# A hybrid attention and retention layer on one core: a reordered opening with lo parts on GpSimd, the samples' values as the stationary side of their product, and a last store cut in parts

## The chip, the cores and the metric

The kernel runs on one NeuronCore of a Trainium2 chip, as one program. The metric is device time of one execution in microseconds (us). Engines are named as in the profile: PE (TensorE, with its weight loads as PEld), DVE (VectorE), ACT (ScalarE), POOL (GpSimd) and SP (SyncE, whose queue issues the DMAs here). Each engine takes its own instructions in the order in which the program gives them and waits where an operand isn't ready.

## What is computed

One layer, one inference step, for a prompt of 512 tokens, 32 sample tokens (8 sequences of 4) and 16 meta tokens, which share all weights. The model width is 2048 and everything is float32. Cut to what matters:

```python
u = einsum('btd,de->bte', rms_norm(h, norm_g), w_in)            # 2048 -> 12800 columns
qa, ka, va, za, qr, kr, vr, zr, ga, gr = split(u)
# A: sliding-window attention, 16 heads of 64, 4 KV heads, learned sinks, 16 meta tokens always visible
p = exp(s - m) / (sum(exp(s - m)) + exp(sink - m));   o_a = p @ v
# B: retention, 8 heads, key 128, value 256, chunks of 128, state S
S_new = exp(c * lg) * S + einsum('bjhd,bjhe->bhde', k * wk, v)
y_a = (o_a * silu(za)) @ w_pa
y_r = ((group_norm(o_r) * gn_g + gn_b) * silu(zr)) @ w_pr
y = h + (sigmoid(ga) * y_a + sigmoid(gr) * y_r) @ w_o
```

A sample's query sees 128 cached keys of its own sequence, the new keys of the samples and the 16 meta tokens. Outputs are `y` for prompt and samples, the last key and value windows, and the retention states. The 48 rows of sample and meta tokens that all samples' products share are called the shared rows below.

## The kernel before

**Numbers in two parts.** A product of float32 matrices is made of three passes over rounded operands: each operand is split into hi (a rounded copy, by ACT) and lo (the rest, by a subtraction, mostly on DVE), and PE adds hi·hi, hi·lo and lo·hi. `split` (L156 to L158) does this for weights (tile `wspl`, 128x512 at a time) and `make_x` for the normed input (`xh`, `xl`, L231 to L244). Some small products run as plain float32, which the trace shows as two PE instructions for each matmul.

**Jobs.** The work is a list of jobs, each of 128 output columns: a job's weights are loaded in two halves (`run_load`, `wraw`), split in four steps (`run_split`), multiplied over 16 blocks k of the contraction (`run_mm`, L471, tile `pproj`), and evacuated. Side work (heads of attention, samples, retention) stands in generators that emit a piece between blocks: `clock` counts the blocks and a `yield n` lets n of them pass. So the order of PE is written by the program: where a piece waits for another engine, everything behind it on PE waits too. Later jobs are pairs that use seven products in place of eight (`Pair`, L410); they are not changed.

**The opening** (`start`, L246). The tokens arrive in five groups: 0 to 3 are 128 prompt tokens each, 4 holds the samples and the meta tokens. A group is squared and summed (`sq`, L208 to L212, two parts on ACT and two on DVE), its scale is formed (`norm`, L218 and L199; the power runs on POOL), and its four parts are scaled (L223 on ACT, L225 on DVE). `make_x(k, half)` transposes block k of groups 0 and 1 (half 0, 256 columns) or 2 to 4 (half 1, 304 columns). The first job `j0` runs half 0 first, while groups 2 to 4 are normed between its blocks by a table `plan`; then come half 1 of three blocks, eight blocks of half 0 of the second job `j1` (`j1.ahead = 8`), and half 1 of `j0`. Six buffers `spl` hold the split weights.

**The heads** (`k_side`, L627; `pair_side`, L680) transpose the keys or queries of two heads: blocks of 128 tokens, then the 32 or 48 rows of samples and meta tokens as a smaller transposition (`pke`, `pqe`), and for the keys three of 16 rows (L638) among the large ones.

**The samples** (`sample_work`, L795; `sample_side`, L844). For each of the 8 sequences, the scores of all heads stand on 128 rows (4 KV groups of 32). Their transposed probabilities are the stationary side, 32 columns for one group at a time: L837 multiplies with the cached values (128 rows), L838 with the shared rows (48 rows), into `spo`. When all are done, `os` copies the sum, four transpositions (`pf`) turn it, and 32 small products on DVE (L875) gate it into `oas`.

**Retention** (`ret_side`, L958). The meta tokens' state is one plain float32 product over 32 rows (L1069, from `kmt` and `vmt`).

**The end** (`out_side`, L1487): two jobs' columns are transposed back (`pout`), the residual is added, and the rows are stored; for the last pair this follows its last step.

Of the kernel before, what the change touches and what calls it, by code (L numbers as in the profile page):

```python
# [15 lines left out]
P = 128  # L16
# [94 lines left out]
def hybrid_step(ctx: ExitStack, tc: tile.TileContext, A, O):  # L111
# [101 lines left out]

    def norm(i):
# [3 lines left out]
        nc.vector.tensor_reduce(out=r, in_=ss[:, i], axis=AX.X, op=ALU.add)  # L218
        rsqrt(r, r, 1.0 / D, 1e-6, 1)
# [26 lines left out]
    def start(j0, j1):  # L246
# [10 lines left out]
        load_ext()  # L257
        load_x(3)
        run_load(j1, 1)
# [5 lines left out]
        for i in range(2):  # L265
            for c in range(4):
                sq(i, c)
            norm(i)
        for j in (j0, j1):
            j.cuts = ((0, 256), (256, TF))  # L270
# [3 lines left out]
        plan = {2: "20 21", 4: "22 23", 6: "n2", 9: "40 41", 10: "42 43", 11: "n4", 14: "30 31", 15: "32 33"}  # L274
        for k in range(NK):
# [4 lines left out]
            for o in plan.get(k, "").split():  # L280
                if o[0] == "n":
                    norm(int(o[1]))
# [12 lines left out]
        for k in range(j1.ahead):  # L295
            run_mm(j1, k, (0,))
        for k in range(NK):
# [3 lines left out]
            if k in (8, 13):  # L301
                run_split(j1, {8: 2, 13: 3}[k])
# [24 lines left out]
    class Job:  # L327
        def __init__(self, w, c0, nk, rhs, n, evac, pre=None, need=None, kdone=None):
            self.w, self.c0, self.nk, self.rhs, self.n, self.evac = w, c0, nk, rhs, n, evac
            self.pre, self.need, self.kdone, self.cuts, self.ahead = pre, need, kdone, None, 0  # L330
            self.banked, self.tile = False, None
# [110 lines left out]
    def run_split(job, s, eng=nc.vector):  # L442
# [5 lines left out]
        wt = spl.tile([P, 2, 4, P], F32R, tag="spl", name="wspl")  # L448
        hi, lo = wt[:, 0], wt[:, 1]
# [177 lines left out]
    def k_side(n, raw):  # L627
# [5 lines left out]
        for i in range(4):  # L633
# [3 lines left out]
            if i < 3:  # L637
                nc.tensor.transpose(o[:, c + P:c + 144], kt[NS:48, 4], ident[NS:48, NS:48])  # L638
        tr(pe[:, :48], kt[:48, 4], 48)
# [40 lines left out]
    def pair_side(i, raw, get_sz):  # L680
# [8 lines left out]
        tr(pe[:, :NS], kt[:NS, 4], NS)  # L689
# [105 lines left out]
    def sample_work(bb, st):  # L795

        for b in range(bb, 8, 2):
# [32 lines left out]
            nc.vector.tensor_copy(PT[:48, P:256], pT[:48, P:256])  # L830
            yield 4
            if "po" not in st:
                st["po"] = psb("spo")
            po = st["po"]
            for g in range(4):
                o = po[32 * g:32 * g + 32, 64 * b:64 * b + 64]
                nc.tensor.matmul(o, PT[:, 32 * g:32 * g + 32], vcv[:, bb, 64 * g:64 * g + 64], start=True, stop=False)  # L837
                nc.tensor.matmul(o, PT[:48, P + 32 * g:P + 32 * g + 32], vx[:, 64 * g:64 * g + 64],  # L838
# [738 lines left out]
```

## Time and profile before

| | |
|---|---|
| median of 3 runs | 1842.52 us (1841.9 to 1843.4) |
| the profiled execution's own time | 1842.39 us |
| its span (first to last instruction) | 1840.5 us |
| PE busy | 1810.9 us, 98% of the span |
| DVE, ACT, POOL busy | 66%, 40%, 9% |

Busy time of PE is modelled, since matmuls overlap; the chain of waits gives an instruction only what it adds to the chain, which is what is used for sums. A group `L837 PE MATMUL spo<-kvc,sPT` reads: line, engine, operation, tile written, tiles read. In the timeline a row ends with the idle time before it and what ended it. PEclk in the table of windows is the share of full TensorE clock that was granted.

### The profile page before, as it was taken

To read this page: it belongs to the slowest core of one execution; us is meant where nothing else is said; L and a number is where in the kernel's file an instruction comes from. 1 tells how busy PE (TensorE), PEld (TensorE's weight loads), DVE (VectorE), ACT (ScalarE), POOL (GpSimd) and SP (SyncE) were. 2 spreads that over 40 slices of the span, in tenths; PEclk is the share of its full clock that TensorE was granted. 3 is DMA by queue.
4 is the path that set the end of the run, shared out by engine and by line. 5 is a ranking of instruction groups with operands and counts; after the bars stand their busy time and mean duration, and the time that the engine had idled before them with its cause. 6 is when DMAs were issued, how large, how long until landed. Compare 5 with 4: busy or idle time off the path is not lost.

```text
span 1840.5 us, 35155 instructions
## 1 busy us (share of the span) xinstructions
PE 1810.9 (98%) x14483; PEld 1767.5 (96%) x14483; DVE 1219.8 (66%) x2191; ACT 731.4 (40%) x1297; POOL 173.5 (9%) x240
## 2 busy tenths in 40 slices
PE   5999999999999999999999999999999999999999
PEld 4999999988999999999999999999999999999998
DVE  5636666645556555545697767777676678799776
ACT  5535555433323222233344444444444333344332
POOL 1100101100223212222000000000000000120000
PEclk8999999999999999999999999999999999999999
DMA  6232133231534443434454554444447764564553
GB/s 189 73 99 64 52 103 85 75 106 42 180 103 130 133 132 110 126 108 137 146 149 141 151 148 126 117 123 127 143 140 251 228 184 146 153 177 129 141 141 96
DMA packets 358368, 239.53 MB, mean 130 GB/s; under 512 B 12320, under 2 KB 332224, under 8 KB 358176
## 3 DMA queue, kind: packets, MB, share of 16 engines
q1 hardware_dynamic: 358208, 237.29, 44.1%
q8 instruction: 114, 1.87, 0.4%
q14 instruction: 46, 0.38, 0.1%
HBM read 197.27 MB, written 41.88 MB: 130 GB/s over the span
## 4 chain that ended last, share of the span: by engine, by line
PE 92%; DVE 3%; DMA 2%; ACT 1%; issue 1%; SPq 1%; POOL 0%; DVEq 0%; ACTq 0%
PE pproj L471 43%; PE pp L410 38%; PE ro L1137 1%; PE pp L471 1%; DVE wspl L158 1%; PE po L764 1%; DMA qdc<-c_qdec 1%; PE pout L154 0%; PE pT L154 0%; DVE ml L158 0%; PE rso L1097 0%; PE px L154 0%; PE rsu L1103 0%; PE psc L721 0%; PE pM L154 0%
## 5 line engine op out<-in xcount | busy, mean ns | idle before, releaser
L471 PE MATMUL pproj<-xh,wspl 128*128 128x272 f32 (+3 forms) x3840 | 714.6, 295 | 2.0 <-ACT xh L242 2.0
L158 DVE TENSOR_TENSOR wspl<-wraw,wspl 128x512 fp32r<-128x512 f32 (+1 forms) x492 | 465.0, 950 | 218.4 <-ACT wspl L157 215.6
L471 PEld LDWEIGHTS pproj<-xh,wspl 128*128 128x128 f32 x3840 | 567.4, 190 | 11.1 <-issue 4.8
L157 ACT ACTIVATE wspl<-wraw 128x512 fp32r<-128x512 f32 (+1 forms) x492 | 389.0, 804 | 371.5 <-DVE wraw L368 156.7
L471 PE MATMUL pproj<-xl,wspl 128*128 128x272 f32 (+3 forms) x1920 | 405.1, 290 | 1.0 <-DVE xl L243 1.0
L471 PEld LDWEIGHTS pproj<-xl,wspl 128*128 128x128 f32 x1920 | 305.4, 189 | 1.8 <-DVE xl L243 1.8
L410 PE MATMUL pp<-xfh,wspl 128*128 128x272 f32 x1280 | 246.2, 287 | 0.0
L410 PEld LDWEIGHTS pp<-xfh,wspl 128*128 128x128 f32 x1280 | 202.7, 188 | 0.0
L410 PE MATMUL pp<-xh,wspl 128*128 128x272 f32 x960 | 187.6, 288 | 0.0
L410 PE MATMUL pp<-xfl,wspl 128*128 128x272 f32 x640 | 162.8, 287 | 0.0
L410 PEld LDWEIGHTS pp<-xh,wspl 128*128 128x128 f32 x960 | 153.0, 188 | 0.0
L410 PE MATMUL pp<-fh,wspl 128*128 128x272 f32 x768 | 146.3, 288 | 0.2 <-ACT wspl L157 0.2
L410 PE MATMUL pp<-xl,wspl 128*128 128x272 f32 x480 | 123.0, 288 | 0.0
L410 PEld LDWEIGHTS pp<-fh,wspl 128*128 128x128 f32 x768 | 121.2, 188 | 0.6 <-ACT wspl L157 0.3
L410 PEld LDWEIGHTS pp<-xfl,wspl 128*128 128x128 f32 x640 | 120.7, 189 | 0.0
L410 PE MATMUL pp<-fl,wspl 128*128 128x272 f32 x384 | 98.1, 288 | 0.0
L410 PEld LDWEIGHTS pp<-xl,wspl 128*128 128x128 f32 x480 | 90.3, 188 | 0.0
L471 PE MATMUL pproj<-fh,wspl 128*128 128x272 f32 x512 | 84.9, 287 | 0.0
L368 DVE TENSOR_TENSOR wraw<-wraw 128x1024 f32<-128x1024 f32 x64 | 78.0, 1219 | 0.0
L410 PE MATMUL pp<-ofh,wspl 128*128 128x272 f32 x384 | 75.3, 290 | 0.0
L410 PEld LDWEIGHTS pp<-fl,wspl 128*128 128x128 f32 x384 | 72.3, 188 | 0.0
L471 PEld LDWEIGHTS pproj<-fh,wspl 128*128 128x128 f32 x512 | 72.2, 188 | 0.0
(314 smaller groups left out, 2445.9 us busy)
## 6 DMA issues: line engine op xcount, KB each, us to landing
wraw<-w_in SPq DMA_DIRECT2D x200, 512.0 KB
wraw<-w_branch_ret SPq DMA_DIRECT2D x32, 512.0 KB
wraw<-w_out SPq DMA_DIRECT2D x32, 512.0 KB
state<-state_ret SPq DMA_DIRECT2D x16, 512.0 KB
o_ret_sample<-state SPq DMA_DIRECT2D x16, 512.0 KB
wraw<-w_branch_attn SPq DMA_DIRECT2D x16, 512.0 KB
m1l<-m_scr SPq DMA_DIRECT2D x20, 272.0 KB
r_scr<-rprime SPq DMA_DIRECT2D x16, 272.0 KB
```

Of the source, the lines that this page charges most:

```text
L157: nc.scalar.activation(out=hi, in_=src, func=AF.Copy)
L158: eng.tensor_tensor(out=lo, in0=src, in1=hi.bitcast(F32), op=ALU.subtract)
L368: eng.tensor_tensor(out=out, in0=a, in1=b, op=ALU.add)
L410: nc.tensor.matmul(job.ps[bank], w[:, k], job.rhs(form, k)[q], start=fresh and i == 0, stop=i == len(seq) - 1, skip_group_check=True)
L471: nc.tensor.matmul(ps[h][:, :c1 - c0], w, x[:, c0:c1], start=a, stop=e)
L764: nc.tensor.matmul(o, src, PT[:, j * 256 + rh:j * 256 + rh + P], start=("s", j) not in st, stop=False, skip_group_check=True)
L1137: nc.tensor.matmul(o, w[:, cs], x, start=q == 0, stop=q == 5)
```

## The change

**The opening.** The second half of `j1`'s weights is loaded before group 3, not after it. The lo parts of `j0`'s last three splits and `j1`'s first three go to POOL. `j1`'s last two splits get buffers of their own (`wspk`, borrowed from the attention's `kk`), so that all four exist before `j0` ends, and all 16 blocks of `j1`'s half 0 run before half 1 begins. A group's scale (`rstd`) is formed apart from its scaling (`norm`), and the table `plan` is new.

**The heads.** The rows of samples and meta tokens are transposed as a full block of 128, and the three small transpositions of the keys follow the large ones.

**The samples.** The values become the stationary side (128 columns: two KV groups at once) and the probabilities move, 32 columns. The shared rows are multiplied once for all samples, from a tile `spx` in which each sample puts its probabilities. The result is already turned, so `os` and `pf` go, and 16 products on DVE replace the 32.

**Retention.** The meta tokens' state comes from three products of hi and lo parts (`kst`, `kml`, `vst`, `vml`).

**The end.** The last pair has its own function, which stores its columns in parts.

```diff
-    def norm(i):
-        n = P if i < 4 else 48
+    def rstd(i):
         r = xrs[:, i:i + 1]
         nc.vector.tensor_reduce(out=r, in_=ss[:, i], axis=AX.X, op=ALU.add)
         rsqrt(r, r, 1.0 / D, 1e-6, 1)
...
         load_ext()
+        run_load(j1, 1)
         load_x(3)
-        run_load(j1, 1)
...
+        j1.spare = 2
...
-        plan = {2: "20 21", 4: "22 23", 6: "n2", 9: "40 41", 10: "42 43", 11: "n4", 14: "30 31", 15: "32 33"}
+        plan = {4: "20 21", 7: "22 23", 9: "r2", 10: "n2 40 41", 12: "42 43", 13: "r4 30 31", 14: "n4 32", 15: "33"}
...
             if k in (1, 5, 8):
-                run_split(j0, {1: 1, 5: 2, 8: 3}[k])
-            if k in (11, 13):
-                run_split(j1, {11: 0, 13: 1}[k])
-        norm(3)
+                run_split(j0, {1: 1, 5: 2, 8: 3}[k], nc.gpsimd)
+            if k in (9, 11, 13):
+                run_split(j1, {9: 0, 11: 1, 13: 2}[k], nc.gpsimd)
+        rstd(3)
         for k in range(NK - LAG, NK):
             run_mm(j0, k, (0,))
+        j1.ahead = 16
+        run_split(j1, 3)
+        norm(3)
+        for k in range(j1.ahead):
+            run_mm(j1, k, (0,))
         for k in range(3):
             make_x(k, 1)
-        j1.ahead = 8
-        for k in range(j1.ahead):
-            run_mm(j1, k, (0,))
...
-            if i < 3:
-                nc.tensor.transpose(o[:, c + P:c + 144], kt[NS:48, 4], ident[NS:48, NS:48])
-        tr(pe[:, :48], kt[:48, 4], 48)
+        tr(pe[:, :P], kt[:, 4])
+        for i in range(3):
+            c = 144 * (i % 2) + P
+            nc.tensor.transpose(pk[i // 2][:, c:c + 16], kt[NS:48, 4], ident[NS:48, NS:48])
...
-        tr(pe[:, :NS], kt[:NS, 4], NS)
+        tr(pe[:, :P], kt[:, 4])
...
-            for g in range(4):
-                o = po[32 * g:32 * g + 32, 64 * b:64 * b + 64]
-                nc.tensor.matmul(o, PT[:, 32 * g:32 * g + 32], vcv[:, bb, 64 * g:64 * g + 64], start=True, stop=False)
-                nc.tensor.matmul(o, PT[:48, P + 32 * g:P + 32 * g + 32], vx[:, 64 * g:64 * g + 64],
-                                 start=False, stop=True)
+            for q in range(2):
+                nc.tensor.matmul(pov[:, q, b], vcv[:, bb, P * q:P * q + P], ptv[:, q, :, 0:16],
+                                 start=first and q == 0, stop=False, skip_group_check=True)
...
+        for q in range(2):
+            nc.tensor.matmul(po[:, 256 * q:256 * q + 256], vx[:, P * q:P * q + P], st["px"][:48, 256 * q:256 * q + 256],
+                             start=False, stop=True, skip_group_check=True)
...
-        nc.tensor.matmul(pu[:, :256], kmt[96:128], vmt[96:128])
+        for q, (w, x) in enumerate(((kst, vst), (kst, vml), (kml, vst))):
+            nc.tensor.matmul(pu[:, :256], w[96:128], x[96:128], start=q == 0, stop=q == 2)
...
+    def out_last(n, y, x):
+        ...
+        yield 3
+        nc.vector.tensor_tensor(out=x[0][:, :512], in0=pt[:, 0], in1=x[0][:, :512], op=ALU.add)
+        nc.sync.dma_start(O["y_prompt"][0, 0:256, cs].rearrange("(b p) c -> p b c", p=P), r3(x[0][:, :512], 256))
+        for j in (1, 0):
+            while not done.get("last") and j == 0:
+                yield 1
+            ...
+            nc.vector.tensor_tensor(out=xv, in0=r3(pt[:, 0, :256], P), in1=xv, op=ALU.add)
+            nc.sync.dma_start(O["y_prompt"][0, 256:512, cs][:, c].rearrange("(b p) c -> p b c", p=P), xv)
+            nc.vector.tensor_tensor(out=x[2][:NS, c], in0=pt[:NS, 1, :P], in1=x[2][:NS, c], op=ALU.add)
+            nc.sync.dma_start(ysm[:, n * P + P * j:n * P + P * j + P], x[2][:NS, c])
...
+            if n == NK - 2:
+                if s == 5:
+                    side_add(out_last(n, t["y"], t["x"]), 4)
+                if s == 6:
+                    done["last"] = True
+            elif s == 6:
                 side_add(out_side(n, t["y"], t["x"]), 4)
```

Three places, as the instructions stand on an engine. First POOL in the opening, from the memory fills to the first head's key norm (`xrs` is a group's scale, `wspl` and `wspk` are lo parts of weights). Before:

```order
L590 MEMSET qz 128x1024
L199 ISA
L199 TENSOR_TENSOR xrs<-xrs,nhalf 128x1 x5
L601 MEMSET kt 128x128
L199 TENSOR_TENSOR rs<-rs,nhalf 128x10
```

And now:

```order
L199 TENSOR_TENSOR xrs<-xrs,nhalf 128x1 x2
L158 TENSOR_TENSOR wspl<-wraw,wspl 128x512 x3
L199 TENSOR_TENSOR xrs<-xrs,nhalf 128x1
L158 TENSOR_TENSOR wspl<-wraw,wspl 128x512 x2
L199 TENSOR_TENSOR xrs<-xrs,nhalf 128x1
L158 TENSOR_TENSOR wspk<-wraw,wspk 128x512
L199 TENSOR_TENSOR xrs<-xrs,nhalf 128x1
L609 MEMSET kt 128x128
```

Six subtractions of 128x512 stand among the powers that give the scales of groups 2, 4 and 3, each of which must run before DVE can scale that group.

Second DVE, from the scaling of group 2 to the first `xl` of half 1. Before:

```order
L225 TENSOR_SCALAR xext<-xext,xrs 48x512 x3
L158 TENSOR_TENSOR wspl<-wraw,wspl 128x512
L243 SCALAR_TENSOR_TENSOR xl<-px,gains,xh 128x256
L158 TENSOR_TENSOR wspl<-wraw,wspl 128x512
L211 SCALAR_TENSOR_TENSOR xjunk,xss<-xin 128x512 x2
L218 TENSOR_REDUCE xrs<-xss 128x1
L198 TENSOR_SCALAR xrs<-xrs 128x1
L225 TENSOR_SCALAR xin<-xin,xrs 128x512 x3
L243 SCALAR_TENSOR_TENSOR xl<-px,gains,xh 128x304 x12
```

And now:

```order
L228 TENSOR_SCALAR xin<-xin,xrs 128x512 x3
L211 SCALAR_TENSOR_TENSOR xjunk,xss<-xext 48x512
L246 SCALAR_TENSOR_TENSOR xl<-px,gains,xh 128x256 x2
L211 SCALAR_TENSOR_TENSOR xjunk,xss<-xext 48x512
L216 TENSOR_REDUCE xrs<-xss 128x1
L198 TENSOR_SCALAR xrs<-xrs 128x1
L211 SCALAR_TENSOR_TENSOR xjunk,xss<-xin 128x512
L228 TENSOR_SCALAR xext<-xext,xrs 48x512 x3
L211 SCALAR_TENSOR_TENSOR xjunk,xss<-xin 128x512
L216 TENSOR_REDUCE xrs<-xss 128x1
L198 TENSOR_SCALAR xrs<-xrs 128x1
L158 TENSOR_TENSOR wspk<-wraw,wspk 128x512
```

The last two `xl` of half 0, which PE's blocks 14 and 15 need, now stand behind the scaling of group 2, and one split stands ahead of the scaling of group 3; the other splits are gone from DVE.

Third PE, the end of one sample's product with the values and what follows it. Before (the pair of L837 and L838 stands four times in a row, once for each KV group; its last time is shown):

```order
L837 MATMUL spo<-kvc,sPT 32x64
L838 MATMUL spo<-vx,sPT 32x64
L154 MATMUL pkc<-ident,kvc 128x128 x2
L471 MATMUL pproj<-xh,wspl 128x280 x2
L471 MATMUL pproj<-xl,wspl 128x280 x2
```

And now:

```order
L849 MATMUL spo<-sPT,kvc 128x32 x2
L154 MATMUL pkc<-ident,kvc 128x128 x2
L479 MATMUL pproj<-xh,wspl 128x280 x2
L479 MATMUL pproj<-xl,wspl 128x280 x2
L479 MATMUL pproj<-xh,wspl 128x280 x2
```

Eight matmuls for each sample, alternating between 128 and 48 rows, became two of 128 rows; the shared rows' two matmuls stand once, behind the last sample.

More of the change, by code (lines that the diff above doesn't have):

```diff
@@ L212, in sq @@
                                            op1=ALU.mult, accum_out=ss[:n, i, c:c + 1])
+    def rstd(i):
+        r = xrs[:, i:i + 1]
+        nc.vector.tensor_reduce(out=r, in_=ss[:, i], axis=AX.X, op=ALU.add)
+        rsqrt(r, r, 1.0 / D, 1e-6, 1)
     def norm(i):
@@ L330, in __init__ @@
             self.pre, self.need, self.kdone, self.cuts, self.ahead = pre, need, kdone, None, 0
-            self.banked, self.tile = False, None
+            self.banked, self.tile, self.spare = False, None, 0
             self.ps, self.raw = None, None
@@ L447, in run_split @@
         src = r3(job.raw[s // 2], P)[:, 4 * (s % 2):4 * (s % 2) + 4]
-        wt = spl.tile([P, 2, 4, P], F32R, tag="spl", name="wspl")
-        hi, lo = wt[:, 0], wt[:, 1]
+        if s < 4 - job.spare:
+            wt = spl.tile([P, 2, 4, P], F32R, tag="spl", name="wspl")
+            hi, lo = wt[:, 0], wt[:, 1]
+        else:
+            hi, lo = (r3(att.tile([P, TF], F32R, tag="kk", name="wspk", bufs=8)[:, :512], P) for _ in range(2))
         split(hi, lo, src, eng)
@@ L849, in sample_side @@
             yield
-        st = {"n": 0}
+        st = {"n": 0, "px": slot(name="spx")}
         for bb in range(2):
@@ L1047, in ret_side @@
             tr(pb[:, n * P:n * P + P], reps[1 + n])
-        vst, vmt = r1k(F32R, "vst"), r1k(name="vmt")
+        vst, vml = r1k(F32R, "vst"), r1k(F32R, "vml")
         nc.scalar.activation(out=vst, in_=pb[:, :256], func=AF.Copy)
@@ L1051, in ret_side @@
         nc.vector.tensor_tensor(out=vst[r], in0=pb[r, :256], in1=vst[r].bitcast(F32), op=ALU.subtract)
-        nc.scalar.activation(out=vmt[96:128], in_=pb[96:128, :256], func=AF.Copy)
+        r = slice(96, 128)
+        nc.vector.tensor_tensor(out=vml[r], in0=pb[r, :256], in1=vst[r].bitcast(F32), op=ALU.subtract)
         px = psb("rx")
@@ L1485, in out_load @@
         return x + [xs]
+    def out_last(n, y, x):
+        cs = slice(n * P, n * P + 256)
+        pt = psmain("pout")
+        for b in range(2):
+            for j in range(2):
+                tr(pt[:, 0, 256 * b + P * j:256 * b + P * j + P], y[j][:, P * b:P * b + P])
+        yield 3
[4 more added lines that the diff above has]
+                yield 1
+            pt = psmain("pout")
+            c = slice(P * j, P * j + P)
+            for b in range(2):
+                tr(pt[:, 0, P * b:P * b + P], y[j][:, 256 + P * b:256 + P * b + P])
+            tr(pt[:NS, 1, :P], y[j][:, SEQ:TC])
+            xv = r3(x[1][:, :512], 256)[:, :, c]
+            nc.vector.tensor_tensor(out=xv, in0=r3(pt[:, 0, :256], P), in1=xv, op=ALU.add)
+            nc.sync.dma_start(O["y_prompt"][0, 256:512, cs][:, c].rearrange("(b p) c -> p b c", p=P), xv)
+            nc.vector.tensor_tensor(out=x[2][:NS, c], in0=pt[:NS, 1, :P], in1=x[2][:NS, c], op=ALU.add)
+            nc.sync.dma_start(ysm[:, n * P + P * j:n * P + P * j + P], x[2][:NS, c])
     def out_side(n, y, x):
```

49 lines of the change are left out of this document (20 added, 29 removed).

## The prediction

> **What bounds the kernel now.** I read the page first, its busy times and its chain of waits, then who waited for whom on PE.
>
> ```profile
> PE 1810.9 (98%) x14483; PEld 1767.5 (96%) x14483; DVE 1219.8 (66%) x2191; ACT 731.4 (40%) x1297; POOL 173.5 (9%) x240
> PE 92%; DVE 3%; DMA 2%; ACT 1%; issue 1%; SPq 1%; POOL 0%; DVEq 0%; ACTq 0%
> ```
>
> ```profile
> PE px L154 <- DVE xin L225: 9.5, 3, 3.3
> PE pproj L471 <- ACT xh L242: 2.0, 1, 2.0
> PE ru L1069 <- ACT vmt L1052: 1.1, 1, 1.1
> ```
>
> PE is the bound: 92% of the chain is its own work, and apart from the opening it waits for almost nothing (1.1 us at the first head's state is the longest). No row names a weight load. So an instruction less on PE is time less, as long as the engines behind it keep up. The opening is different. The timeline of PE there, and the granted clock of two stretches in the table of windows (start and end, width, then busy times, then PEclk):
>
> ```profile
> 25.66 0.44 PE L154 MATMUL px<-ident,xin 128*128 128x128 f32 x2 [1.80 <-DVE xl L243]
> 31.59 0.39 PE L471 MATMUL pproj<-xh,wspl 128*128 128x256 f32 x1 [2.02 <-ACT xh L242]
> 35.89 0.47 PE L154 MATMUL px<-ident,xin 128*128 128x128 f32 x1 [2.93 <-DVE xin L225]
> 43.41 0.53 PE L471 MATMUL pproj<-xh,wspl 128*128 128x256 f32 x2
> 43.78 0.30 PE L471 MATMUL pproj<-xl,wspl 128*128 128x304 f32 x1
> 43.92 0.30 PE L471 MATMUL pproj<-xh,wspl 128*128 128x304 f32 x1
> ```
>
> ```profile
> 19.80:33.30 13.50, 8.37 (x60) 6.92 (x58) 12.04 (x33) 9.94 (x25) 1.10 (x2) 1.00 0.83 222
> 33.50:43.50 10.00, 7.61 (x32) 6.46 (x33) 3.90 (x11) 2.26 (x4) 0.70 (x2) 0.50 0.19 55
> ```
>
> Three gaps, 6.75 us together, and the clock at 0.50 for 10 us after the second: 7.61 us of work there cost about 3.8 us extra. DVE was busy 12.04 of 13.5 us in the stretch with the gaps: PE waits for it. The first 304-column product, where `j0`'s half 1 begins, is the second of the two in the row of 43.41, at about 43.6 us.
>
> **The opening.** DVE's price for a lo part and for a scaling in the first 64 us, POOL's for the same subtraction, and the one place where both work on SBUF at once:
>
> ```profile
> L158 DVE TENSOR_TENSOR wspl<-wraw,wspl 128x512 fp32r<-128x512 f32 x10 | 6.9, 688 | 0.7 <-ACT wspl L157 0.7
> L225 DVE TENSOR_SCALAR xin<-xin,xrs 128x512 f32<-128x512 f32 x12 | 5.1, 482 | 2.8 <-POOL xrs L199 2.8
> ```
>
> ```profile
> L1027 POOL TENSOR_TENSOR innl<-inn,innh 128x512 fp32r<-128x512 f32 x8 | 10.3, 1288 | 15.6 <-ACT innh L1026 15.6
> ```
>
> ```profile
> 478.40 1.29 POOL L1029 TENSOR_TENSOR qdl<-qd,qdh 128x512 fp32r<-128x512 f32 x1
> ```
>
> ```profile
> 478.68 1.55 DVE L158 TENSOR_TENSOR wspl<-wraw,wspl 128x512 fp32r<-128x512 f32 x1 [0.35 <-ACT wspl L157]
> ```
>
> Half 1 starts with the transposition at 35.89, which waited for DVE's first scaling of group 3. Ahead of that scaling DVE had five splits behind `j0`'s first, and now has one: four at 0.69 less, 2.8 us, so 33.1 if nothing holds DVE. Something will: six POOL subtractions of 1.29 us. The last two rows show a DVE subtraction with both operands in SBUF that starts 0.28 us after POOL's and takes 1.55 in place of 0.69 us: it sits until POOL is done. In the opening the squares, the scalings and the last split read SBUF alone. No row shows a scaling under a POOL subtraction; the bounds are no hold (0) and all six (7.7 us). I take three, 3.9 us, because on POOL a subtraction stands right behind the powers of groups 2 and 4, and so starts together with the scaling that such a power releases. [...]
>
> That puts the first transposition at 37.0. Nine of them at 0.11 to 0.26 and the first `xh` and `xl` (about 0.5, a scaling's price) make 1.7 us until the first 304-column product: 38.7 in place of 43.6, 4.9 gained. By then `j1` has eight blocks more behind it, 24 matmuls at 0.12 (L1079's row of 256 columns below): 2.9. One loss follows, because `j1`'s blocks are now all half blocks, and the generators count blocks:
>
> ```profile
> 60.45 9.82 PE pproj L471 x75
> ```
>
> ```profile
> 68.01 0.33 DVE L625 TENSOR_TENSOR kt<-rt,rt 128x160 f32<-128x160 f32 x1
> ```
>
> The first key head's tile was ready at 68.34, 7.9 us after PE left `pta` at 60.45; PE asked for it after 9.82 us. In the new order 51 matmuls lie between, 39 of 304 columns (0.14, from 43.78 to 43.92) and 12 at 0.13: 7.0 us. PE waits 0.9 us. Opening: **-6.9**; bounds from -10 (no hold) to -1.5 (all six held, and the half clock again). That group 3 is loaded later hides behind the norming of groups 2 and 4, since its first square stands after block 13; uncovered it costs the other load's 0.5 MB at the 222 GB/s of that stretch (the last column), 2.4 us.
>
> **The samples.** The chain gives, for one sample and for nearby plain float32 and rounded products:
>
> ```profile
> 382.12 0.23 PE spo L837 x2
> 382.35 0.23 PE spo L838 x2
> ...
> 383.94 0.37 PE pkc L154 x2
> ```
>
> ```profile
> 367.44 0.22 PE pkc L154 x2
> 370.89 0.35 PE pss L807 x8
> ```
>
> ```profile
> 532.68 0.22 PE rx L1054 x2
> 535.99 0.62 PE ru L1069 x2
> 538.35 0.12 PE ru L1079
> ```
>
> One sample costs 382.12 to 383.94, 1.82 us for 16 instructions, and 0.15 on the transposition behind it (0.37 against 0.22), which comes after the change back from 48 to 128 rows: 1.97. Now a sample has two matmuls of full shape, four instructions, and no change of rows. The price of one lies between L807's 0.044 (32 columns loaded, 128 moved, four groups side by side) and `rx`'s 0.11 (128 loaded, 128 moved); 32 move now, but 128 are loaded, so I take `rx`'s: 0.44. [...] Eight samples save 12.2 (up to 14.3). The shared rows' two products are nearest to L1069 (0.62 for one of 256 columns over 32 rows; 0.15 of it the change of rows, as above): 0.15 + 2 x 0.47 + 0.15 = 1.2. The four `pf` go (0.44). **-11.4.**
>
> **Heads and state.**
>
> ```profile
> 70.38 0.16 PE pk L638
> 70.54 0.26 PE pk L154
> 71.64 0.19 PE pke L154
> ```
>
> ```profile
> 363.62 1.52 PE pproj L471 x12
> 365.57 0.17 PE pqe L154
> 365.74 1.70 PE pproj L471 x12
> ```
>
> Keys: 70.27 to 71.83 is 1.56 for eight transpositions; now five large ones at 0.11 (two `pkc` take 0.22) and three small ones after one change, 0.16 and twice 0.05 (as L807's), 0.81. Twice: **-1.5**. Queries: 0.17 and 0.18 on what follows (1.70 against 1.52), now 0.11 and nothing: 0.24, eight times: **-1.9**. State: 0.62 becomes 0.15 + 3 x 0.12 = 0.51, eight times: **-0.9**. The 1.1 us wait at the first state has its chain in `oas`: 32 DVE products before, 16 now, and one block earlier; I take it as gone, **-1.0** (bound 0).
>
> **The end.**
>
> ```profile
> 1836.37 0.69 DVE L1499 TENSOR_TENSOR xres<-pout,xres 128x512 f32<-128x512 f32 x1 [0.28 <-PE pout L154]
> 1837.57 0.41 SPq L1504 DMA_DIRECT2D o_y_sample<-xs  x1
> ```
>
> The new function is entered with a delay of four counts at the end of step 5, and step 6 counts four: its first piece stands behind the last product, as before. So nothing is stored earlier; DVE has two short additions more and SP five issues of 0.41 in place of three. The last issue ends about 0.3 us later: **+0.3** (-0.2 to +0.8).
>
> Sum: -6.9 - 11.4 - 1.5 - 1.9 - 0.9 - 1.0 + 0.3 = -23.3. From the profiled execution's 1842.39 (the runs' median is 1842.52) that is 1819.1; I forecast **1819**.
>
> **The rivals.**
>
> *The half clock comes again.* Before, it came at about 33.4, after gaps of 1.80 and 2.02 us and within the third. Now the last two `xl` of half 0 wait behind group 2's scaling, which gives PE a gap of about 1.5 us, and as much again if POOL holds DVE. If the clock halves at about 30 us for 10 us, PE loses 5 us, part of which it would have waited: opening -3.5, time 1822.5. For it: the gaps lie as close as before. Against it: all 16 blocks of `j1` fill what was idle later. [...] Chance 0.3.
>
> *The value products are dear.* Their moving side is picked in pieces of 16 columns. If an instruction costs what L1069's does without the change of rows (0.235, 256 columns moved), a sample takes 0.94 and the samples save 7.5 in place of 11.4: 1823. Against it: a price of 256 columns for 32. Chance 0.04.
>
> *No hold on DVE.* Scalings pass POOL and the products move at 0.05: opening -10, samples -13.4: 1814. For it: no row shows a scaling held. Chance 0.14.
>
> *Slower.* The clock stays at half for the whole rebuilt opening. The rest of the change gains 16.4; the opening would have to lose that, so half clock would have to last 33 us beyond the gaps, against 10 before; at 40 us the time is 1846. [...] Chance 0.02. *The change doesn't shorten the samples*, because their chain on ACT and DVE sets the pace and PE waits instead: then about 1830.5; but 36 products lie between scores and transposition as before, and DVE is busy two thirds of the time. Chance 0.04.
>
> **How the numbers follow.** My forecast has 0.46 and its own range 1816 to 1822. With the half clock and the dear products the range reaches 1828, with no hold 1814: low 1814, high 1828. About 0.2% (3.7 us) is what a measurement can tell from no change: faster by more 0.96, within 0.02, slower 0.02.
>
> **What would show it.** Right: the first 304-column product at about 38 us, the granted clock at 1.00 from 20 us on, `spo` at 0.11 an instruction, no 0.37 behind it, `pqe` without the 0.18, the last issue no earlier behind the last product. Wrong: DVE scalings at 0.48 while POOL subtracts (no hold), a stretch at 0.50 between 30 and 40 us, or `spo` rows waiting for `sPT` or `spx`. The forecast fails if PE, freed of 16 us of work in the heads and samples, shows that much new idle time in front of any one tile.

## The result

The changed kernel takes 1823.67 us (median of four runs, 1823.2 to 1824.0) against 1842.92 for the kernel before (four runs, 1841.9 to 1843.4): the ratio is 0.9896, with a 95% interval of 0.9879 to 0.9913, or 19.2 us less. The forecast was 1819, the range 1814 to 1828. The profiled execution took 1824.02 us, 18.4 less than the one profiled before, and its span is 1822.1.

### The profile after

The page's busy times, then, of who waited for whom on PE, the rows that bear on the change (us in total, times, longest), both of the changed kernel:

```profile
PE 1793.6 (98%) x14395; PEld 1761.4 (97%) x14395; DVE 1220.4 (67%) x2178; ACT 727.9 (40%) x1289; POOL 183.4 (10%) x246
```

```profile
PE px L154 <- DVE xin L228: 6.6, 2, 3.3
PE pT L154 <- DVE ptile L748: 2.1, 3, 1.4
PE pproj L479 <- ACT xh L245: 1.3, 1, 1.3
PE pproj L479 <- DVE xl L246: 1.2, 1, 1.2
PE pproj L479 <- DVE wspk L158: 1.1, 1, 1.1
PE rx L1060 <- POOL qpad L1026: 1.0, 1, 1.0
PE pk L154 <- DVE kt L633: 1.0, 1, 1.0
PE rke L154 <- POOL rep L991: 0.5, 1, 0.5
```

PE has 17.3 us less to do and is still the bound. The list of waits is new: one at half 1's first transposition is gone (`px` waits twice, not three times), `ru` no longer waits, but `pT`, `rx`, `pk`, `rke` and `wspk` do. Each of them is one tile at one place.

The timeline of PE in the opening, and the two windows of it that the prediction looked at:

```profile
28.00 0.38 PE L479 MATMUL pproj<-xh,wspl 128*128 128x256 f32 x1 [1.33 <-ACT xh L245]
29.59 0.38 PE L479 MATMUL pproj<-xl,wspl 128*128 128x256 f32 x1 [1.21 <-DVE xl L246]
36.35 0.50 PE L479 MATMUL pproj<-xh,wspk 128*128 128x256 f32 x2 [1.07 <-DVE wspk L158]
37.63 0.38 PE L154 MATMUL px<-ident,xin 128*128 128x128 f32 x2
39.25 0.41 PE L479 MATMUL pproj<-xh,wspl 128*128 128x304 f32 x1
64.11 0.66 PE L154 MATMUL pk<-ident,kt 128*128 128x128 f32 x4 [0.95 <-DVE kt L633]
```

```profile
19.80:33.30 13.50, 10.96 (x86) 10.49 (x84) 11.31 (x28) 10.89 (x27) 8.03 (x8) 1.00 0.91 235
33.50:43.50 10.00, 8.89 (x57) 7.06 (x57) 7.13 (x17) 4.54 (x11) 1.15 (x3) 1.00 0.36 97
```

The gaps are three again, but 3.6 us together in place of 6.75, and the granted clock is 1.00 in both windows. Half 1's first 304-column product starts at 39.25, where 43.6 stood before.

Where the 18.4 us come from is read by taking the same instruction in both traces and subtracting its starts. The gain up to each, and what each stage adds:

| up to the start of | before | after | gain so far | this stage | forecast |
|---|---|---|---|---|---|
| first key tile's transposition | 70.11 | 64.11 | 6.00 | opening 6.0 | 6.9 |
| the third job's transposition behind the keys | 123.92 | 116.59 | 7.33 | keys 1.3 | 1.5 |
| first sample's transposition | 367.28 | 357.94 | 9.34 | queries 2.0 | 1.9 |
| first retention head's transposition | 465.06 | 445.65 | 19.41 | samples 10.1 | 11.4 |
| first state's product | 481.75 | 462.84 | 18.91 | waits there -0.5 | 1.0 |
| last head's last `ro` | 902.77 | 883.26 | 19.51 | states 0.6 | 0.9 |
| last eviction of the gates' pairs | 1380.28 | 1361.94 | 18.34 | branches' products -1.2 | 0 |
| last product's addition | 1834.96 | 1816.41 | 18.55 | 0.2 | 0 |
| end of the span | 1840.5 | 1822.1 | 18.4 | end -0.1 | -0.3 |

The forecast was 4.9 us too good in all: 0.9 in the opening, 1.3 in the samples, 1.5 at the first state, 0.3 in the states and 1.0 in a stage that the change doesn't touch.

### The profile page after: what moved, and what is told of

It is laid out like the page before. It is cut to its first block, busy times and chain, and to the rows that moved or that the text cites. A ratio compares the mean times of both kernels' runs of the same rounds, so it can differ in the third digit from the quotient of the medians.

```text
span 1822.1 us, 34970 instructions
## 1 busy us (share of the span) xinstructions
PE 1793.6 (98%) x14395; PEld 1761.4 (97%) x14395; DVE 1220.4 (67%) x2178; ACT 727.9 (40%) x1289; POOL 183.4 (10%) x246
## 4 chain that ended last, share of the span: by engine, by line
PE 91%; DVE 3%; DMA 2%; ACT 2%; issue 1%; SPq 0%; POOL 0%; DVEq 0%; ACTq 0%; POOLq 0%
PE pproj L479 43%; PE pp L415 39%; PE ro L1144 1%; PE pp L479 1%; DMA xin<-x_prompt 1%; DVE wspl L158 1%; PE po L773 1%; DMA qdc<-c_qdec 1%; PE pout L154 0%; PE pT L154 0%; DVE ml L158 0%; PE rso L1104 0%; PE rsu L1110 0%; PE pM L154 0%; PE psc L730 0%
## 5 line engine op out<-in xcount | busy, mean ns | idle before, releaser
L158 DVE TENSOR_TENSOR wspl<-wraw,wspl 128x512 fp32r<-128x512 f32 (+1 forms) x485 | 459.5, 952 | 207.6 <-ACT wspl L157 204.9
L479 PEld LDWEIGHTS pproj<-xh,wspl 128*128 128x128 f32 x3808 | 560.9, 189 | 8.6 <-issue 2.5
L479 PE MATMUL pproj<-xl,wspl 128*128 128x272 f32 (+3 forms) x1904 | 400.7, 290 | 1.2 <-DVE xl L246 1.2
L373 POOL TENSOR_TENSOR wsum<-wraw 128x1024 f32<-128x1024 f32 x2 | 4.8, 2392 | 705.5 <-DVE wspl L158 705.5
```

The costliest lines, as they stand in the source:

```text
L158: eng.tensor_tensor(out=lo, in0=src, in1=hi.bitcast(F32), op=ALU.subtract)
L373: eng.tensor_tensor(out=out, in0=a, in1=b, op=ALU.add)
L479: nc.tensor.matmul(ps[h][:, :c1 - c0], w, x[:, c0:c1], start=a, stop=e)
```

## The experiments

Single times below are of one execution; medians and intervals are against runs of the kernel before on the same chip. The gains at a tile are differences of starts, as in the table.

### The samples' part alone

The diff, on the kernel before, is the part of the change between `sample_work` and the store of `oas`, and nothing else.

> The kernel before with the samples' part of the change alone (values as stationary side, shared rows once, 16 products into oas); opening, keys, queries, state and end as before. Theory 1, the parts add up and the new wait belongs to the samples: eight samples shorter by 1.55 us each (12.4), the four pf transpositions gone (0.4), the shared rows' products 1.3 more, and a new wait of about 1.4 us before the last block's transposition pT: 10.1 us gained, about 1832.8 us. Theory 2, the wait before pT comes only from the shifted opening: no such wait here, 11.5 us gained, about 1831.4. For the slower products in the pairs of the gates (21.08 in place of 21.03 us for two pairs, 1.15 us in all): if they belong to the samples' part they are here, and 1.1 us less is gained.

1833.68 us, ratio 0.9951 (0.9936 to 0.9966). PE's waits in this kernel:

```profile
PE pT L154 <- DVE ptile L739: 2.1, 3, 1.4
PE rx L1048 <- POOL qpad L1015: 0.9, 1, 0.9
PE rke L154 <- POOL rep L982: 0.5, 1, 0.5
```

The three new waits at `pT`, `rke` and `rx` are here too, though the opening is the old one. So they come with the samples' part, and theory 1 holds, 0.9 us short of its time: PE, with less to do, catches up with DVE at the last attention block, with POOL's padded copies at `rke`, and with a table at `rx`. Up to the last `po` it gains 9.7 us more than at the first key tile; the changed kernel gains 9.6 between its first sample and the same place.

### The opening's part alone

The diff is the change of `start`, `norm` and `run_split`, on the kernel before.

> The kernel before with the opening's part alone (new order of norming, six lo parts on GpSimd, all 16 blocks of j1's half 0 ahead). Theory 1, the parts add up: the first key tile's transposition 6.0 us earlier, as in the changed kernel, clock at 1.00 from 21 us on: about 1836.9 us. Theory 2, the forecast's 6.9 and something that the other parts take back: 1836.0. If the slower products of the gates' pairs belong to the opening, 1.1 us less: 1838.0.

1835.59 us, ratio 0.996 (0.9946 to 0.9974), so 7.4 us by the medians, near theory 2's 6.9; executions ran from 1834.9 to 1839.4, too wide to tell 6.0 from 6.9. The profiled one is the slowest, 1839.38, and shows why it is (windows, the column before the last two is PEclk):

```profile
28.70:35.20 6.50, 5.96 (x28) 5.96 (x29) 5.78 (x17) 3.49 (x9) 3.40 (x3) 0.50 0.80 211
66.20:69.50 3.30, 3.30 (x14) 2.93 (x15) 2.20 (x7) 2.65 (x7) 0.00 (x0) 0.50 0.06 17
```

The clock is halved twice, behind the same gaps as in the changed kernel (1.33 us ahead of 27.65, 0.95 ahead of 64.82), where the changed kernel's profiled execution kept 1.00. So the rival of the half clock is alive: with this opening it comes in some executions and not in others. More on that below.

### The products into `oas` in another order

```diff
-        for g in range(4):
-            for m in range(4):
+        for g, m in [(2 * q + b, 2 * e + d) for b in range(2) for d in range(2) for q in range(2) for e in range(2)]:
                 d = slice(64 * (m % 2), 64 * (m % 2) + 64)
```

> The changed kernel with the 16 products into oas in another order: four at a time that read the same half of the partitions and write the same half. Theory 1, DVE overlaps an operation with the next only if both use the same partitions (before: 32 of them at 0.096 from start to start, ordered by halves; now 16 at 0.196, changing the half at each): 16 at about 0.10 to 0.11, 1.7 us in place of 3.15; the store, the table loaded behind it and the queries' padding come 1.4 us earlier, the waits of 0.47 us at rke and 0.99 us at rx go: about 1.4 us faster, 1822.3. Theory 2, the price goes by columns (32 at 0.19, 16 at 0.096): still 3.15 us, both waits stay, no change, 1823.7.

1822.28 us. DVE's rows of the kernel before, the changed one and this one:

```profile
456.81 3.14 DVE L875 TENSOR_TENSOR oas<-pf,szs 64x16 f32<-64x16 f32 x32
```

```profile
437.84 3.21 DVE L879 TENSOR_TENSOR oas<-spo,szs 64x32 f32<-64x32 f32 x16
```

```profile
437.71 2.02 DVE L878 TENSOR_TENSOR oas<-spo,szs 64x32 f32<-64x32 f32 x16
```

Half as many products took as long as before, and the same products in another order 1.2 us less: 0.20 from start to start where the output's half of the partitions changes at each, 0.12 where it changes every fourth. Theory 1. The wait at `rke` is gone, that at `rx` is 0.2. The rows of DVE show the overlap: before, a product lasted 0.17 us and the next started 0.10 behind it, with eight in a row on one half; in the changed kernel it is 0.19 and 0.20.

### The sum of the denominators by one-column scalars

```diff
-        nc.vector.tensor_tensor(out=sums, in0=sums, in1=es, op=ALU.add)
+        for j in range(2):
+            nc.vector.tensor_scalar(out=sums[:, j:j + 1], in0=sums[:, j:j + 1], scalar1=es[:, j:j + 1],
+                                    scalar2=None, op0=ALU.add)
```

> The changed kernel with the sum of the softmax denominators (sums + es, 128x2) made by two one-column scalar additions on DVE in place of one addition of two SBUF tiles. Theory 1, the 1.33 us that it takes in the last samples' block is a hold by POOL's rotary sum that runs beside it, and only an operation with two SBUF tiles as inputs is held: the two take 0.15 each there, the transposition pT is released about 1.1 us earlier, its wait falls from 1.45 to about 0.3: 1822.6 us. Theory 2, any DVE operation on SBUF is held, or what was late is the exponential on ACT: the first one takes 1.2 us as before, the wait stays, 1823.7.

1824.74 us, over what either theory gave. In the changed kernel the wait of 1.45 us at `pT` has this behind it, on DVE and on POOL:

```profile
426.31 1.33 DVE L745 TENSOR_TENSOR sums<-sums,es 128x2 f32<-128x2 f32 x1
427.88 0.63 DVE L748 TENSOR_SCALAR ptile<-ptile,sums 128x272 f32<-128x272 f32 x2
```

```profile
425.70 1.92 POOL L957 TENSOR_TENSOR rot<-rot,rtmp 128x560 f32<-128x560 f32 x1 [16.68 <-DVE rtmp L956]
```

An addition of 128x2 (the median of its 32 is 0.16 us) lasts until POOL's rotary sum is done, at 427.6. With the scalars:

```profile
426.79 0.32 DVE L746 TENSOR_SCALAR sums<-sums,es 128x1 f32<-128x1 f32 x2
427.34 1.18 DVE L750 TENSOR_SCALAR ptile<-ptile,sums 128x272 f32<-128x272 f32 x2
```

The one-column scalars are not held, and the scaling behind them is, 1.18 in place of 0.63: the hold went to the operation behind them, while POOL's sum ran from 426.19 to 428.10. The wait at `pT` fell to 0.99 only, and the longer chain showed at two earlier blocks (`pT` at 140.7 and 143.0, 0.69 and 0.49 us, where the changed kernel waits 0.52 and 0.15).

### The sum ahead of the rotary products

```diff
-        yield D2
+        yield D2 - 1 if (i, blk) == (7, 3) else D2
...
-        yield D3
+        yield D3 + 1 if (i, blk) == (7, 3) else D3
```

> The changed kernel with the last block's sum of denominators, its reciprocal and its two scalings moved on DVE ahead of the first rotary products (and so ahead of POOL's rotary sum); PE's order is the same. Theory 1, the new wait of 1.45 us at pT comes from that place in DVE's order (2.2 us of rotary products, a split and a hold of 1.2 us stand before it): the wait goes, 1.4 us gained, 1822.3. Theory 2, the wait only goes over to the next tile, since the chain of a_scr and of the table behind it starts from po and was late anyway: the wait at rx grows by as much: 1823.7.

1822.22 us; no wait at the last `pT`, `rke` and `rx` wait 0.46 and 0.85 as before. Theory 1: the wait was one place in DVE's order, with nothing behind it to take the gain back.

### The lo parts of the opening back on DVE

```diff
-                run_split(j0, {1: 1, 5: 2, 8: 3}[k], nc.gpsimd)
+                run_split(j0, {1: 1, 5: 2, 8: 3}[k])
...
-                run_split(j1, {9: 0, 11: 1, 13: 2}[k], nc.gpsimd)
+                run_split(j1, {9: 0, 11: 1, 13: 2}[k])
```

> The changed kernel with the six lo parts of the opening back on DVE, order as changed. In the changed kernel's trace POOL's subtractions stretch DVE's three scalings of group 2 from 1.28 to 2.28 us, those of the last rows from 1.28 to 2.30, and a square from 0.67 to 0.96: 2.3 us of holds. Theory 1, the forecast's account: six splits of 0.69 come back (4.1 us), 2.3 us of holds go: DVE ends its opening 1.8 us later, first transposition of half 1 at 39.4 in place of 37.6, about 1825.5 us. Theory 2: DVE was idle 1.4 us in gaps between 20 and 26 us, and PE waits there for the pace of xh and xl, so the splits fit in: first transposition at 37.0 to 37.6, 1823.0 to 1823.7 us.

1823.64 us, ratio 0.9892 (0.9878 to 0.9907), where the changed kernel's is 0.9896 (0.9879 to 0.9913): no difference in the time, as theory 2 has it: moving six subtractions to POOL did not gain. The equal times are not the whole account, though. In this trace the first scaling of group 3 starts 0.84 us earlier than in the changed kernel (36.74, below):

```profile
35.90 1.28 DVE L228 TENSOR_SCALAR xin<-xin,xrs 128x512 f32<-128x512 f32 x3 [0.44 <-POOL xrs L199]
```

PE could not use it, since it ran at half clock from 31.0 to 34.4: its first transposition of half 1 stands at 37.97 for 37.63, and the first key tile 0.3 us later. On the other side the gates' products are 0.76 us faster in this kernel, for a reason that stays open (see the end). What the move to POOL costs DVE stands in the changed kernel, DVE's scalings and POOL's subtractions at the same times:

```profile
26.25 2.28 DVE L228 TENSOR_SCALAR xin<-xin,xrs 128x512 f32<-128x512 f32 x3
32.32 2.30 DVE L228 TENSOR_SCALAR xext<-xext,xrs 48x512 f32<-48x512 f32 x3 [0.44 <-POOL xrs L199]
36.74 1.28 DVE L228 TENSOR_SCALAR xin<-xin,xrs 128x512 f32<-128x512 f32 x3 [0.44 <-POOL xrs L199]
```

```profile
26.19 1.26 POOL L158 TENSOR_TENSOR wspl<-wraw,wspl 128x512 fp32r<-128x512 f32 x1
28.54 1.72 POOL L158 TENSOR_TENSOR wspl<-wraw,wspl 128x512 fp32r<-128x512 f32 x1 [1.09 <-ACT wspl L157]
32.25 1.29 POOL L158 TENSOR_TENSOR wspk<-wraw,wspk 128x512 fp32r<-128x512 f32 x1
```

Two of three groups of scalings are held 1.0 us each, and POOL pays too, 1.72 for 1.28 beside a square on DVE (0.67 us from 28.45). The profiled execution of the kernel with the lo parts on DVE, 1825.08, also shows the half clock far from the opening, behind the wait at `pT` (windows):

```profile
427.00:430.00 3.00, 1.55 (x12) 1.38 (x12) 2.15 (x5) 0.60 (x1) 1.57 (x3) 1.00 0.00 0
430.40:433.60 3.20, 3.20 (x13) 2.55 (x12) 0.00 (x0) 0.00 (x0) 0.00 (x0) 0.50 0.00 0
```

One gap of 1.45 us, and then 3.4 us at half clock, which cost 1.5 us more between `pT` and the last `po` than in the changed kernel.

### The last stores earlier

```diff
-                    side_add(out_last(n, t["y"], t["x"]), 4)
+                    side_add(out_last(n, t["y"], t["x"]), 1)
```

and `yield 1` in place of `yield 3` ahead of the first addition.

> The changed kernel with out_last entered with a delay of one count in place of four and one count in place of three ahead of its first addition, so that two of its three pieces really stand among the last product's matmuls. Theory 1, after the last product DVE and SP work in a row: the first piece's addition (0.69) and three of five issues (0.4 each) leave the end, while the last piece still waits for the last product's addition (0.44): last issue at about 2.9 us behind the last product in place of 3.6 and PE does 0.8 us of transpositions before it in place of behind it: about 0.5 us gained, 1823.2. Theory 2, what ends last is only the last piece's own chain: no change, 1823.7.

1824.53 us: no gain in the time. From the last product's addition to the end of the span it took 4.5 us in place of 5.7, but that product came 0.8 us later behind seven transpositions: about 0.4 us of gain at the end, where theory 1 has 0.5. In this execution `ru` waited 0.93 us for `vml` and took more than that away; the same wait stands in the trace of the one-column scalars and in no other.

### The norming gathered behind half 0

```diff
-        plan = {4: "20 21", 7: "22 23", 9: "r2", 10: "n2 40 41", 12: "42 43", 13: "r4 30 31", 14: "n4 32", 15: "33"}
+        plan = {0: "s01", 3: "22 21 23 s02 t03", 7: "41 20 r2", 9: "s10", 12: "43", 13: "t11", 14: "t12",
+                15: "t13 42 30 40 n2", 16: "32 r4 31 33 r3 n3 n4"}
```

(`s` is a split with its lo part on POOL, `t` one on DVE; 16 is behind half 0.)

> The changed kernel with another order of the opening: lo parts 1 and 2 of j0 and 0 of j1 on GpSimd, the others on DVE, and the norming of groups 2, 4 and 3 together behind the last blocks of half 0. Theory 1, PE's gaps of 1.33 and 1.21 us come from norming that stands ahead of the last xh and xl, and POOL's holds fall on scalings only because they are started side by side: half 0 runs without a gap over 0.3 us, one gap of 1 to 2 us is left ahead of half 1, first transposition of half 1 at about 33 in place of 37.6, 3 to 4 us gained: 1820. Theory 2, the loads of group 3 (issued from 18.65 us) or the sum of DVE's work set it: first transposition at 37, 1823.5. With the granted clock halved in a gap: 1 to 3 us less than theory 1.

1824.17 us, ratio 0.9893 (0.9876 to 0.9909), single executions 1822.7 to 1832.1. The order did most of what it should: half 1's first transposition stands at 34.12, 3.5 us earlier than in the changed kernel, with one gap of 0.85 us behind it, at 35.56. But a gap of 1.43 us, at 23.6, stayed within half 0, where theory 1 had none. Then, in the profiled execution (1832.11):

```profile
25.00:35.00 10.00, 9.71 (x80) 9.18 (x78) 9.10 (x28) 7.64 (x19) 3.44 (x5) 1.00 0.90 251
37.20:60.90 23.70, 23.70 (x84) 17.84 (x83) 7.77 (x15) 6.95 (x14) 0.00 (x0) 0.50 0.08 23
61.10:66.00 4.90, 4.90 (x38) 4.89 (x38) 1.71 (x3) 3.28 (x7) 0.00 (x0) 1.00 0.00 0
```

PE is busy without a break for 24 us, at half clock, behind a gap of 0.85 us. Half of that, 12 us, is lost; the other executions of this kernel took 8 to 9.5 us less.

### The waits taken out together

```diff
+        if h == 0:
+            copy_windows()
```

in `ret_side` behind the states' loads, in place of the call ahead of it; the order of `oas`, the early sum and the early stores from above; and the keys' `yield 6` ahead of their transpositions made 7.

> The changed kernel with the four small moves together: products into oas by partition halves, the last block's sum ahead of the rotary products, the two window copies (1 MB each) issued behind the first retention head's tables and states in place of ahead of them, out_last entered three counts earlier, and the first key heads' transpositions one count later. Theory 1, each wait was a matter of its own place: oas 1.4 us, pT 1.4, what is left at rx 0.2, pk 0.75, end 0.4: 4.1 us gained, 1819.5 us; the table qdc lands within 4 us of its issue in place of 13.1, because the window copies were ahead of it in the queue. Theory 2, what is freed is taken back at the next tile of the retention (ru waiting for vml about 0.9 us, as in two of the runs before): 1820.5 to 1821; if the copies are not what holds the table, it still takes 12 to 13 us.

1820.03 us, ratio 0.9873 (0.9858 to 0.9887). No wait is left at the last `pT`, `rke`, `rx` or `ru`; at the first key tile 0.6 us of 0.95 stays. Theory 1, 0.5 us short; the last pairs' products, which were not touched, took 0.6 us longer here than in the changed kernel. What had held the table is seen in the changed kernel's chain, and in this kernel's rows of SP and POOL:

```profile
443.89 13.12 DMA qdc<-c_qdec
457.00 0.07 issue
457.07 1.30 POOL qd L1022
```

```profile
440.49 0.43 SPq L977 DMA_DIRECT2D qdc<-c_qdec  x1
```

```profile
443.93 1.29 POOL L1022 TENSOR_TENSOR qd<-rot,qdc 128x512 f32<-128x512 f32 x1
```

64 KB took 13.1 us behind two copies of 992 KB on the same queue, and at most 3.4 ahead of them.

### The gaps of the opening filled

```diff
+        def fill(n):
+            for _ in range(n):
+                nc.tensor.matmul(j0.ps[1][:, :256], j0.wsp[0][0][:, 0], XH[0][:, 0:256], start=True, stop=True)
...
+        fill(20)
         for k in range(NK - LAG, NK):
...
+            if k == 12:
+                fill(9)
             run_mm(j1, k, (0,))
```

> The kernel of the run waits_removed, with PE's gaps in the opening filled by products whose result is never read: 20 ahead of the last two blocks of half 0 (2.4 us where PE waits 1.33 and 1.21), 9 ahead of block 12 of j1 (1.07). They write a bank that is begun anew afterwards. Theory 1, the granted clock is halved for one or several periods of 3.4 us when PE idles for about 1 us in one of them: now no halved stretch in any run, mean clock 0.999 to 1.000 in all, the runs within 0.6 us of each other, the median 0 to 1.5 us under the other kernel's, as often as it was halved. Theory 2, the halving does not come from idle time (load, or chance): halved as often, same time, same spread; then the filling costs up to 0.5 us.

1820.0 us, ratio 0.9874 (0.9859 to 0.9888): no gain, and no loss by 29 products more. The profiled execution has no halved stretch in the opening, where the kernel without the filling had one of 3.4 us from 30.1. So in these two traces the clock follows theory 1. The mean clocks (1.000 in three of the four filled executions, 0.999 in all four of the others) add little: the last 2 us of a span, where PE has nothing to do, are at half clock too, and give 0.999 by themselves, in the changed kernel and in the filled one. The short halved stretch there cost nothing that the medians show (1820.03 and 1820.0 us), since PE would have waited for `wspk` anyway (1.07 us in the changed kernel). The spread did not shrink (1819.8 to 1821.0).

### The gathered norming, filled and not filled

The gathered plan on the kernel of the waits taken out, with `fill(12)` ahead of the transposition that waited 1.43 us and `fill(10)` ahead of half 1's first; then the same without the two calls.

> The kernel of the run waits_removed with the gathered norming of the run opening_gathered, and its gaps filled in the same way (12 products ahead of the transposition at 23.6 us that waited 1.43, 10 ahead of half 1's first). Theory 1, what took back the gathered order's gain was the halved clock (24 us in its profiled run, clock 0.999 in the others), and idle time brought that: no halved stretch, first 304-column product about 2.5 us earlier than in the changed kernel: 1817 us. Theory 2, the halving comes whether PE idles or not: 1820 to 1828 us.

> The kernel of the run gathered_filled without its 22 filling products: the small moves and the gathered norming alone. Theory 1, the filling is what kept the granted clock up: mean clock under 1.000 in most runs, a halved stretch behind the gap ahead of half 1, 1.7 us for each period of 3.4 us beyond what PE would have waited: 1819.5 to 1821 us, single runs up to 1828. Theory 2, the gain of gathered_filled over gaps_filled (2.2 us) comes from the order and from the gates' products, which were not slower there: 1817.8 us here too, clock 1.000.

Filled: 1817.79 us, ratio 0.9859 (0.9843 to 0.9876), executions 1817.1 to 1818.2, mean clock 1.000 in all. Not filled: 1819.72, ratio 0.9883 (0.9864 to 0.9902), executions 1816.9 to 1828.6, mean clock 0.992 and 0.993 in the two at 1828.6 and 1827.4, 1.000 in three. The same windows of both, not filled first:

```profile
25.00:35.00 10.00, 9.99 (x83) 9.46 (x81) 9.09 (x28) 7.64 (x19) 3.46 (x5) 1.00 0.87 237
37.30:64.20 26.90, 26.90 (x95) 21.04 (x96) 7.95 (x15) 7.86 (x16) 0.00 (x0) 0.50 0.14 40
```

```profile
25.00:35.00 10.00, 10.00 (x86) 9.89 (x86) 9.10 (x28) 7.40 (x19) 3.44 (x5) 1.00 0.83 234
37.30:64.20 26.90, 26.35 (x172) 22.68 (x171) 15.10 (x31) 13.22 (x27) 2.48 (x2) 1.00 0.16 44
```

172 rows of matmuls against 95 in the same 26.9 us. Theory 1 for the bad executions, theory 2 for the good ones: without a halving both take about 1818, and the filling's worth is that it did not come. Four clean executions against three of five are no proof by themselves; with the pair before, none of eight filled executions has a mean clock under 0.999, and two of nine unfilled have. Of the 1.9 us between the medians 0.65 can be the gates' products, which were faster in the filled kernel (411.41 us for 412.06, below). The filling has a price: half 1's first 304-column product stands at 37.98, where the kernel without it has 37.15. And the 12 products filled nothing: a gap of 1.66 us, at 24.66, stayed behind them. It halved nothing, so the length of a gap alone does not decide.

The filled kernel is the fastest here, 5.9 us under the changed one by the medians. Its profiled execution is 2.5 us shorter than that of the filled kernel of the old order, and only 0.9 of this is in the opening (first key tile at 63.06 for 63.99); 1.15 is that the gates' products were not slower in it (below), and 0.5 that the last pairs' were not.

## Why the prediction was right or wrong

The sign, the range and the two large terms were right; one term, the first state, had the wrong sign, and the forecast's own span of 1816 to 1822 was missed by 1.7 us.

**The opening, 6.0 for 6.9.** The first transposition of half 1 came at 37.63, where 37.0 was forecast, and the first 304-column product at 39.25 for 38.7. The holds exist, and as "wrong" was listed scalings at 0.48 under POOL: they took 2.28 and 2.30 for three. But "three holds of 1.29" was 1.0 twice and 0.3 for a square. What was missed in its place is that POOL is slowed as well: the last powers take 0.93 and 0.95, where 0.55 to 0.57 stood before, and the squares of group 3 stand behind the held scalings of the last rows. (The powers take 0.93 to 0.95 with all six lo parts on DVE too, so this comes from the squares and splits that the new order puts beside them on DVE: in the changed kernel a square of 0.68 from 31.19 and a split of 0.69 from 35.61.) That POOL brings 2.8 us of splits off DVE's path was the step that failed: with all six back on DVE its first scaling of group 3 came 0.84 us earlier and not later, since DVE had room for them before and nothing held its scalings. The new wait at the first key tile came as forecast, 0.95 for 0.9.

**The half clock.** No stretch at 0.50 in the profiled execution, as forecast; but with this opening, not filled, it came in five of seven other traces, where the rival had 0.3. Its price was overrated, for the reason that the rival half names: at 30 to 34 us PE had a wait of 1.07 us in stock.

**The samples, 10.1 for 11.4.** The chain of the changed kernel:

```profile
372.82 0.36 PE spo L849 x4
373.18 0.25 PE pkc L154 x2
```

```profile
429.75 1.06 PE spo L868 x4
430.81 1.70 PE pproj L479 x12
```

0.09 an instruction where `rx`'s 0.11 was taken, and 0.03 in place of 0.15 behind it: 1.55 us less for a sample on average, 12.4 in all, for 12.2. The shared rows cost 1.3 (1.06, and 0.15 to 0.2 on the products behind) for 1.2, and the `pf` brought 0.4. The term that was missing is the wait of 1.45 at the last `pT`. The rival "their chain on ACT and DVE sets the pace" came nearest to it, and was set aside because 36 products lie between. But the chain that sets it is that of the last attention block beside the samples, with other work of DVE in it: three rotary products, a split and a hold by POOL. That PE, freed of work, would show new idle time in front of a tile was listed as a way to fail; it came, at 1.45 us at most.

**The first state, -0.5 for 1.0.** "32 DVE products before, 16 now" was counted by instructions; the order of their partitions set the price, and 3.2 us stayed 3.2. The wait of 1.11 at `ru` became 0.47 at `rke` and 0.99 at `rx`.

**Keys 1.3, queries 2.0, states 0.6** for 1.5, 1.9 and 0.9: the state's three products took 0.55 for 0.51.

**The end, 0.1 later** for 0.3: the last issue stands no earlier behind the last product, as said. Entered earlier, it gains about 0.4.

**The branches' products, 1.2 us lost** where nothing changed. That was in no case of the forecast.

## What to carry to other kernels

When PE is the bound and loses work, look at each place where it will catch up with another engine, and ask what stands there on that engine by chance: here four such places took 3.9 us (1.45, 0.47, 0.99 and 0.95), and three of them went by two moves, the early sum and the order of the products into `oas`. A count of instructions was no price on DVE here: the order of the partitions that neighbours write made a product into `oas` 0.12 or 0.20 us, and POOL's rotary sum at the same time made an addition last 1.33 in place of 0.15, nine times as long. A short idle gap ahead of a long stretch of PE work can be worth filling with useless products, since here the clock was halved for 27 us behind a gap of 0.85 us in one execution; the filling was worth at most 1.9 us by the medians in one kernel and nothing in the other.

## What the runs showed of the hardware

**The granted clock was halved for whole periods of 3.4 us.** Seen were one period (3.4 us), two, three, seven and eight, most of them beginning 0.8 to 2 us behind the end of a gap of 0.85 to 2.0 us (in the samples alone within one), and in other executions with the same gaps none. Part of what looks like chance is where the edges of the periods fall. In each trace all changes of the clock lie whole periods of 3.41 us behind its first coming up (at 20.88 us in the changed kernel, where the row of a product of 256 columns goes from 0.41 to 0.28 us). In the eight traces with this opening, not filled, the clock behind the edge that follows its first two gaps goes by how long PE was busy in the period before that edge:

| trace | period, us | PE busy in it, us | clock behind it |
|---|---|---|---|
| waits taken out | 26.72 to 30.14 | 1.15 | 0.50 |
| another order of `oas` | 27.16 to 30.57 | 1.45 | 0.50 |
| the opening alone | 25.18 to 28.59 | 1.52 | 0.50 |
| lo parts back on DVE | 27.62 to 31.03 | 1.68 | 0.50 |
| early sum | 27.70 to 31.11 | 1.78 | 0.50 |
| changed kernel | 27.71 to 31.12 | 1.92 | 1.00 |
| early stores | 27.79 to 31.20 | 1.97 | 1.00 |
| one-column scalars | 27.87 to 31.29 | 2.12 | 1.00 |

With the gaps filled this period has 2.96 us of work, which is what the filling does. Busy time alone is no rule for every place: earlier periods with 1.61 to 1.76 us halved nothing (the kernel before, the samples alone, the last filled one), and 2.56 us, with products in only 0.83 of them, halved it in the gathered kernel. Whether the busy time counts or where in the period the gaps lie is not separated. PE at work did not bring the clock back at once: PE was busy all through 27 us at 0.50 in the gathered kernel, not filled, and for two whole periods, 36.81 to 43.63 us, in the kernel before. Transpositions take 11.7 us of the 27; no run tests by itself whether that plays a part.

**The same products, 0.3% slower.** From the gates' first to their last eviction, in the kernel before and in the changed one:

```profile
968.77 0.40 ACT L418 ACTIVATE gy<-pp 128x272 f32<-128x272 f32 x1 [1.44 <-PE pp L410]
1380.28 0.40 ACT L425 ACTIVATE gy<-pp 128x272 f32<-128x272 f32 x1 [1.68 <-PE pp L410]
```

```profile
949.38 0.40 ACT L423 ACTIVATE gy<-pp 128x272 f32<-128x272 f32 x1 [1.44 <-PE pp L415]
1361.94 0.40 ACT L430 ACTIVATE gy<-pp 128x272 f32<-128x272 f32 x1 [1.85 <-PE pp L415]
```

411.51 us and 412.56, growing evenly, at full clock and with no waits. The difference of 1.05 stands in seven kernels with the changed opening, 0.3 to 0.55 in four others, and none in the opening alone and in the last filled one. Neither part of the change alone brings it in full, and what does stays open.

**POOL and DVE held each other.** In the changed kernel, beside a POOL subtraction or sum of two SBUF tiles, a DVE addition of two SBUF tiles (0.15 became 1.33) and the first of three scalings from SBUF to SBUF (1.28 became 2.30 for the three) ended only behind it; two `xl`, which read PSUM, did not wait (0.86 us for both from 29.07, beside the subtraction of 28.54 to 30.26), nor did the one-column scalars in their run (0.32 us for both). Which of the two engines began first does not settle it: POOL's subtraction of 28.54, 0.09 us behind a square on DVE, took 1.72 where 1.28 is usual; but the split of 128x512 that starts on DVE at 425.71, 0.01 us behind POOL's rotary sum, takes 0.67 us, no longer than alone, and it is POOL's sum that takes 1.92 us, where the shortest of its size takes 1.38.
